# Low parts of one weight tile in eight by an accumulating DMA in a transformer block kernel

## The chip, the cores and the metric

The kernel runs on one core of one Trainium2 chip. The metric is the device time of one execution in microseconds. Two runs of the kernel before took 1663.89 and 1665.68 us, a median of 1664.79 us. The engines are named as in the profile: PE is TensorE (PEld its weight loads), DVE is VectorE, ACT is ScalarE, POOL is GpSimd, SP is SyncE, which here issues loads and stores. A name with a q behind it (SPq, ACTq) is the engine's own instruction queue.

## The reference, cut to what matters

One decoder layer for 256 tokens of width 2048, all in float32. Every large step is a product of the activations with a weight matrix; the parts between them are small.

```
h = rmsnorm(x, ln_mix)                               # x: 256 x 2048
z = h @ w_in                                         # 2048 x 14336: u,v | q,k,v | gates
y_a = spatial_gating_mixer(u, v) @ w_proj_a          # 2048 x 2048
y_b = moba_mixer(q, k, v, rel_bias) @ w_proj_b       # 2048 x 2048
x = x + (sigmoid(g_a) * y_a + sigmoid(g_b) * y_b) @ w_out
h = rmsnorm(x, ln_mlp)
x = x + square(relu(h @ w_up)) @ w_down              # 2048 x 8192, 8192 x 2048
out = rmsnorm(x, ln_final)
```

## The kernel before

All weights together are cut into 288 tiles of 512 rows by 512 columns (1 MB in float32, held as 128 partitions by 2048 elements). Four tiles one below the other make a chunk, which is one product over 2048 rows; there are 72 chunks. Their order is fixed by the list `chunks`: three products (k, q, v) for each of four groups of heads, then the gate of the attention branch (gb), its projection (pb), the spatial branch's v (gv) and u, its projection (pa) and gate (ga), the output projection (wo), and four times four chunks of the MLP's first matrix (up) and four of its second (dn). Tiles are counted through from 0 to 287; tile j belongs to chunk j // 4.

Each float32 weight w is used as two parts of a shorter type (float32r), w = hi + lo, and the activations likewise. A product then takes three matmuls in place of one: hi weights with hi activations, lo weights with hi activations, hi weights with lo activations. In `rows` (L141 to L143), where the activations are the stationary operand, the three follow each other for each block of 128 rows, so that the second matmul of a tile already reads lo. In `cols` (L158), where the weights are stationary, four matmuls with hi and hi, four with hi and the low activations, and then four with lo follow each other for each block of 128 rows, so the first eight matmuls of a tile read hi alone.

`WeightStream` brings the tiles. `load` (L56) issues a DMA from SP into a tile `wraw`, of which there are four buffers. `split` makes hi by a copy with rounding on ACT (L72) and lo by a subtraction on DVE (L73); there are three buffers of `whi` and three of `wlo`. So the split of tile j waits until PE is done with tile j - 3, and the load of tile j + 4 waits until the split of tile j has read `wraw`. The last tile alone puts its parts into separate tiles named `spare`. `get`, called ahead of each tile's matmuls, issues loads up to five tiles ahead and splits up to two tiles ahead. The small work between the products (attention heads, norms, gates) is issued in stages, one or two per weight tile, by `tick`. A scheduler of the language sets the final order of each engine's instructions and the semaphores between engines; each engine then runs its own list in order.

Of the kernel before, what the change touches and what calls it, by code (L numbers as in the profile page):

```python
# [12 lines left out]
F32 = mybir.dt.float32  # L13
F32R = mybir.dt.float32r
AF = mybir.ActivationFunctionType
ALU = mybir.AluOpType
AX = mybir.AxisListType

P = 128
D = 2048  # L20
T = 256
NT = T // P
KT = D // P
# [5 lines left out]
EPS = 1e-6  # L29
NEG = -1e30  # L30
SCALE = P ** -0.5
CH = 512
KG = 4
RV = 384


class WeightStream:
    """Weights in tiles of KG*128 rows by CH columns, laid out as in_tiles() does, each split exactly into two float32r parts:
    w = hi + lo. Loads and splits are issued ahead of the products that use them."""

    def __init__(self, nc, pool, chunks, ahead=2, loads_ahead=5):
        self.nc, self.pool = nc, pool
# [17 lines left out]
    def split(self, pieces=None, between=None):  # L60
        j = self.n_split
        t = self.raw.pop(j)
        if j == len(self.tiles) - 1 and self.spare:
            hi, lo = self.spare
        else:
            hi = self.pool.tile([P, KG, CH], F32R, tag="whi", name=f"whi{j}", bufs=3)
            lo = self.pool.tile([P, KG, CH], F32R, tag="wlo", name=f"wlo{j}", bufs=3)
        for a, b in pieces or (((0, 2), (2, 4)) if j < 6 else ((0, KG),)):
            if between:
                between(a, b)  # L70
            s = slice(a, b)
            self.nc.scalar.activation(hi[:, s], t[:, s], AF.Copy)  # L72
            self.nc.vector.tensor_tensor(lo[:, s], t[:, s], hi[:, s].bitcast(F32), ALU.subtract)  # L73
        self.parts[j] = (hi, lo)
        self.n_split += 1

# [11 lines left out]
def block_kernel(ctx, tc, x, x_t, ln_mix, w_in, v_gain, w_sp, b_sp, w_pa, w_pb, w_out, rel_bias,  # L88
# [23 lines left out]
        chunks += [(w_up, 0, b * D + c * CH) for c in range(4)]  # L112
        chunks += [(w_down, b * D, c * CH) for c in range(4)]

# [1 line left out]
    tasks = deque()  # L116

    def tick(limit=2):
# [10 lines left out]
    stream = WeightStream(nc, wpool, chunks)  # L129

    def rows(acts, name):
        """[tokens, CH] = acts.T @ W over 2048 rows, both token tiles."""
        ps = psum.tile([P, NT, CH], F32, tag="mm", name=name, bufs=2)
        for i in range(KT // KG):
            hi, lo = stream.get()
            for kk in range(KG):
                k = i * KG + kk
                ah, al = acts(k)
                for t in range(NT):
                    s = slice(t * P, (t + 1) * P)  # L140
                    nc.tensor.matmul(ps[:, t], ah[:, s], hi[:, kk], start=k == 0, stop=False)  # L141
                    nc.tensor.matmul(ps[:, t], ah[:, s], lo[:, kk], start=False, stop=False)  # L142
                    nc.tensor.matmul(ps[:, t], al[:, s], hi[:, kk], start=False, stop=k == KT - 1)  # L143
            if i < KT // KG - 1:
                tick()
        return ps

    def cols(acts, name):
        """[CH as 4 x 128, tokens] = W.T @ acts over 2048 rows."""
        ps = psum.tile([P, CH // P, T], F32, tag="mm", name=name, bufs=2)  # L150
        for i in range(KT // KG):
            hi, lo = stream.get()
            for kk in range(KG):
                k = i * KG + kk
                ah, al = acts(k)
                for j, (w, a) in enumerate(((hi, ah), (hi, al), (lo, ah))):
                    for n in range(CH // P):
                        nc.tensor.matmul(ps[:, n], w[:, kk, n * P : (n + 1) * P], a,  # L158
                                         start=k == 0 and j == 0 and n % 2 == 0,
                                         stop=k == KT - 1 and j == 2, skip_group_check=True)  # L160
            if i < KT // KG - 1:
                tick()
        return ps

# [1 line left out]
    ident = const.tile([P, P], F32, name="ident")  # L166
    make_identity(nc, ident)
    ones = const.tile([P, P], F32, name="ones")
# [17 lines left out]
    first = [((0, 1), (1, 2), (2, 3), (3, 4))] * 2 + [((0, 2), (2, 4))] * 2  # L186
# [4 lines left out]
    hh = hold.tile([P, KT, T], F32R, tag="h", name="hh", bufs=2)  # L191
# [10 lines left out]
        split_x(k)  # L202

    def rsqrt(dst, s, n, scale=1.0):
        """dst = (scale * s + EPS) ** -0.5, the table's root refined by a Newton step."""
        v = const.tile([P, n], F32, tag="rs_v", name="rs_v", bufs=2)
        y = const.tile([P, n], F32, tag="rs_y", name="rs_y", bufs=2)
        q = const.tile([P, n], F32, tag="rs_q", name="rs_q", bufs=2)
        nc.vector.tensor_scalar(v, s, scale, EPS, op0=ALU.mult, op1=ALU.add)
        nc.scalar.activation(y, v, AF.Sqrt)  # L210
        nc.vector.reciprocal(y, y)
        nc.vector.tensor_mul(q, y, y)
        nc.vector.tensor_mul(q, q, v)
        nc.vector.tensor_scalar(q, q, -0.5, 1.5, op0=ALU.mult, op1=ALU.add)
        nc.vector.tensor_mul(dst, y, q)

    def row_of(r, name):
        """r [token, 2] on every partition as a row [*, 256]."""
        ps = psum.tile([P, T], F32, tag="tp", name=name + "p", bufs=2)
        for t in range(NT):  # L220
            dg = const.tile([P, P], F32, tag="diag", name="dg", bufs=2)
            nc.vector.tensor_scalar(dg, ident, r[:, t : t + 1], None, op0=ALU.mult)
            nc.tensor.matmul(ps[:, t * P : (t + 1) * P], ones, dg, start=True, stop=True)
        rb = const.tile([P, T], F32, tag="rb", name=name, bufs=2)
        nc.vector.tensor_copy(rb, ps)
        return rb
# [22 lines left out]
    tasks.append(first_norm())  # L249

    def split_t(dst_h, dst_l, k0, src):
        """Two transposed blocks [128, 2, 256] in PSUM -> hi and lo parts of k0, k0 + 1."""
        nc.scalar.activation(dst_h[:, k0 : k0 + 2], src, AF.Copy)
        nc.vector.tensor_tensor(dst_l[:, k0 : k0 + 2], src, dst_h[:, k0 : k0 + 2].bitcast(F32),
                                ALU.subtract)

    def transpose_pair(src, k, name):
        """Blocks k, k + 1 (of 128 columns) of src [tokens, ...] -> PSUM [128, 2, 256]."""
        tp = psum.tile([P, 2, T], F32, tag="tp", name=name, bufs=2)
        for a in range(2):  # L260
            for t in range(NT):
                nc.tensor.transpose(tp[:, a, t * P : (t + 1) * P],
                                    src[:, t, (k + a) * P : (k + a + 1) * P], ident)
        return tp

# [1 line left out]
    bh = bl = None  # L267
    with tc.tile_pool(name="attn", bufs=1) as at:
        rv = at.tile([HEADS, RV], F32, tag="pt", name="rv", bufs=2)
# [53 lines left out]
            nc.scalar.activation(bh[:, h], pv, AF.Copy)  # L323
            nc.vector.tensor_tensor(bl[:, h], pv, bh[:, h].bitcast(F32), ALU.subtract)

        hacts = lambda k: (hh[:, k], hl[:, k])  # noqa: E731

        def scale_cols(ps, name):
            dst = at.tile([P, 4, T], F32, tag=name[:2], name=name, bufs=2)
# [23 lines left out]
                tasks.append(head(c, j, qt, kt, vt, bt))  # L353
            tick()

# [1 line left out]
        m = hold.tile([P, NT, D], F32, tag="m", name="m", bufs=1)  # L357
        for c in range(4):
            ps = rows(hacts, f"gb{c}")
# [4 lines left out]
        drain()  # L364

    with tc.tile_pool(name="gmlp", bufs=1) as gp:
# [1 line left out]
        for c in range(4):  # L368
            ps = rows(lambda k: (bh[:, k], bl[:, k]), f"pb{c}")
            for t in range(NT):  # L370
                s = m[:, t, c * CH : (c + 1) * CH]
                nc.vector.tensor_tensor(s, s, ps[:, t], ALU.mult)

# [1 line left out]
        gain = gp.tile([P, GROUPS], F32, name="gain")  # L375
        nc.sync.dma_start(gain, v_gain)
        gv = gp.tile([P, NT, D], F32, tag="gv", name="gv", bufs=1)
# [62 lines left out]
            for t in range(NT):  # L440
                nc.scalar.activation(pa[:, t, c * CH : (c + 1) * CH], ps[:, t], AF.Copy)

# [1 line left out]
        mh = ab.tile([P, KT, T], F32R, tag="ab", name="mh", bufs=2)  # L444
        ml = ab.tile([P, KT, T], F32R, tag="ab", name="ml", bufs=2)

# [13 lines left out]
                nc.vector.tensor_tensor(m[:, t, s], m[:, t, s], g[:, t], ALU.add)  # L460
            tasks.append(merged(c))

# [1 line left out]
    lnp = const.tile([P, KT], F32, name="lnp")  # L464
    nc.sync.dma_start(lnp, ln_mlp)
    x1 = hold.tile([P, NT, D], F32, tag="m", name="x1", bufs=1)
# [7 lines left out]
    r2 = const.tile([P, NT], F32, name="r2")  # L474

    def add_rows(ps, t, s, sums=None):
        """x1 += ps in columns s of token tile t; sums gets the sum of the squares."""
        xs = x1[:, t, s]
        nc.vector.tensor_tensor(xs, xs, ps, ALU.add)
        if sums is not None:  # L480
            jk = const.tile([P, CH], F32, tag="junk", name="jk", bufs=2)
            nc.scalar.activation(jk[:, : s.stop - s.start], xs, AF.Square, accum_out=sums)
# [24 lines left out]

    ab_open.close()

# [1 line left out]
    mlp = ctx.enter_context(tc.tile_pool(name="mlp", bufs=1))  # L511
    lnf = mlp.tile([P, D], F32, name="lnf")
    nc.sync.dma_start(lnf, bass.AP(tensor=ln_final.tensor, offset=ln_final.offset,
# [1 line left out]
    for b in range(DFF // D):  # L515
        hid = []
        for c in range(4):
# [10 lines left out]
                nc.scalar.activation(q, v, AF.Square)  # L528
                nc.vector.tensor_tensor(tl[:, s], q, th[:, s].bitcast(F32), ALU.subtract)
            hid.append((th, tl))  # L530
        acts = lambda k: (hid[k // 4][0][:, k % 4], hid[k // 4][1][:, k % 4])  # noqa: E731
        last = b == DFF // D - 1
        for c in range(3 if last else 4):
            ps = rows(acts, f"dn{b}_{c}")
# [5 lines left out]
                else:  # L540
                    add_rows(ps[:, t], t, s)

# [1 line left out]
    spare = [hold.tile([P, KG, CH], F32R, tag="h", name=f"spare{i}", bufs=2) for i in range(2)]  # L544
    stream.spare = tuple(spare)
    out_v = out.rearrange("(t p) d -> t p d", p=P)
# [42 lines left out]


def in_tiles(w):
    """[rows, cols] as [row tile, column tile, 128, KG, CH]: each weight tile in one piece."""
    r, c = w.shape
    return np.asarray(w).reshape(r // (KG * P), KG, P, c // CH, CH).transpose(0, 3, 2, 1, 4)


def _onehot():
    """Which bucket a distance of 255 - m falls in, for m < 256; the rest is masked."""
    n = np.arange(256)
    half = BUCKETS // 2  # L600
    large = half + (np.log(np.maximum(n, 1).astype(np.float32) / np.float32(half))
# [45 lines left out]
```

## Time and profile before

| what | value |
|---|---|
| runs before, median of 2 | 1664.79 us (1663.89 to 1665.68) |
| span of the profiled execution | 1662.5 us |
| PE busy | 1651.6 us, 99% |
| DVE busy | 850.9 us, 51% |
| ACT busy | 688.8 us, 41% |
| POOL busy | 4.3 us |
| read from HBM | 311.50 MB, 190 GB/s over the span |
| hardware DMA queue (SP) | 53.9% of 16 engines' time |
| queue of DMAs issued by POOL | 32 packets, 0.01 MB |

The span runs from the first to the last instruction of one execution that the hardware profiler took, 2.3 us less than the median of the runs. Busy time of an engine says how long its instructions ran, not whether anybody waited for them; the waits and the timeline say that. A load's time to landing is counted from its issue to the moment its semaphore says that the data is there. The share of the DMA engines is a mean over the whole span.

### The profile page before, as it was taken

The page shows a single profiled execution, that of the slowest core. Times are in us where ns is not written, and L with a number is a line of the kernel's source. Part 1 is how long each engine was busy: PE and PEld are TensorE (multiplying, and loading weights), DVE is VectorE, ACT ScalarE, POOL GpSimd, SP SyncE. Part 2 cuts the span into 40 slices and gives each one's busy share as a digit, 9 for nine tenths or more (in the row PEclk, how much of TensorE's full clock was granted, in tenths as well). Part 3 has the DMA queues.
Part 4 walks back from the last instruction along what each step waited for, and adds up shares of the span by engine and source line. Part 5 has one row for each costly group of instructions (what it writes and reads, how often), then busy time and mean ns, then how long its engine had stood idle before and what let it go on. Part 6 is the DMA issues. An engine that isn't in the chain of part 4 may idle for free.

```text
span 1662.5 us, 22670 instructions
## 1 busy us (share of the span) xinstructions
PE 1651.6 (99%) x9988; PEld 1483.7 (89%) x9988; DVE 850.9 (51%) x726; ACT 688.8 (41%) x614; POOL 4.3 (0%) x11
## 2 busy tenths in 40 slices
PE   9999999999999999999999999999999999999997
PEld 9899999888888899888888999889988998899986
DVE  7545544544445555544555555444545455445554
ACT  7444343443334443434444444334443443334432
POOL 0000000000000000000000000000000000000000
PEclk9999999999999999999999999999999999999999
DMA  9855444465555554555465554555555555555551
GB/s 317 254 193 187 165 178 170 159 223 185 200 192 189 192 199 169 184 191 202 178 234 189 210 178 178 202 189 191 178 186 194 190 190 178 201 181 186 190 183 74
DMA packets 51762, 317.16 MB, mean 191 GB/s; under 512 B 5664, under 2 KB 10832, under 8 KB 14928
## 3 DMA queue, kind: packets, MB, share of 16 engines
q1 hardware_dynamic: 51632, 315.71, 53.9%
q8 instruction: 78, 1.28, 0.3%
q14 instruction: 20, 0.16, 0.0%
q0 software_dynamic: 32, 0.01, 0.0%
HBM read 311.50 MB, written 4.19 MB: 190 GB/s over the span
## 4 chain that ended last, share of the span: by engine, by line
PE 99%; DMA 0%; DVE 0%; ACT 0%; issue 0%; DVEq 0%; POOL 0%; POOLq 0%; ACTq 0%
PE up L158 22%; PE dn L142 7%; PE dn L143 7%; PE dn L141 7%; PE kt L158 6%; PE qt L158 6%; PE u L158 6%; PE v L142 2%; PE wo L143 2%; PE ga L143 2%; PE gb L141 2%; PE wo L141 2%; PE ga L141 2%; PE wo L142 2%; PE pa L141 2%; PE v L141 2%
## 5 line engine op out<-in xcount | busy, mean ns | idle before, releaser
L73 DVE TENSOR_TENSOR wlo<-wraw,whi 128x2048 fp32r<-128x2048 f32 (+2 forms) x297 | 658.9, 2219 | 644.8 <-ACT whi L72 644.8
L72 ACT ACTIVATE whi<-wraw 128x2048 fp32r<-128x2048 f32 (+2 forms) x297 | 551.5, 1858 | 832.6 <-PE up L158 188.9
L141 PE MATMUL dn<-whi,hh 128*128 128x512 f32 x480 | 186.8, 389 | 0.0
L142 PE MATMUL dn<-wlo,hh 128*128 128x512 f32 x480 | 186.8, 389 | 0.0
L143 PE MATMUL dn<-whi,hl 128*128 128x512 f32 x480 | 186.7, 389 | 0.0
L158 PE MATMUL up<-h2h,whi 128*128 128x256 f32 x1024 | 164.7, 283 | 0.0
L158 PE MATMUL up<-h2l,whi 128*128 128x256 f32 x1024 | 164.6, 283 | 0.0
L158 PE MATMUL up<-h2h,wlo 128*128 128x256 f32 x1024 | 164.6, 283 | 0.0
L158 PEld LDWEIGHTS up<-h2h,whi 128*128 128x128 f32 x1024 | 141.5, 192 | 0.3
L158 PEld LDWEIGHTS up<-h2h,wlo 128*128 128x128 f32 x1024 | 141.3, 192 | 0.0
L158 PEld LDWEIGHTS up<-h2l,whi 128*128 128x128 f32 x1024 | 141.3, 192 | 0.0
L143 PEld LDWEIGHTS dn<-whi,hl 128*128 128x128 f32 x480 | 90.1, 188 | 18.7
L141 PEld LDWEIGHTS dn<-whi,hh 128*128 128x128 f32 x480 | 90.1, 188 | 18.6
L142 PEld LDWEIGHTS dn<-wlo,hh 128*128 128x128 f32 x480 | 90.1, 188 | 18.6
L141 PE MATMUL gb<-whi,hh 128*128 128x512 f32 x128 | 50.6, 395 | 0.0
L141 PE MATMUL wo<-whi,mh 128*128 128x512 f32 x128 | 50.6, 395 | 0.0
L141 PE MATMUL ga<-whi,hh 128*128 128x512 f32 x128 | 50.4, 394 | 0.0
L141 PE MATMUL v<-whi,hh 128*128 128x512 f32 x128 | 50.0, 391 | 0.0
L141 PE MATMUL pa<-whi,ah 128*128 128x512 f32 x128 | 50.0, 391 | 0.0
L143 PE MATMUL wo<-whi,ml 128*128 128x512 f32 x128 | 50.0, 390 | 0.0
L142 PE MATMUL v<-wlo,hh 128*128 128x512 f32 x128 | 50.0, 390 | 0.0
L143 PE MATMUL ga<-whi,hl 128*128 128x512 f32 x128 | 49.9, 390 | 0.0
(180 smaller groups left out, 2394.8 us busy)
## 6 DMA issues: line engine op xcount, KB each, us to landing
wraw<-in_w_in SPq DMA_DIRECT2D x108, 1024.0 KB, 4.8
wraw<-in_w_up SPq DMA_DIRECT2D x64, 1024.0 KB, 4.8
wraw<-in_w_down SPq DMA_DIRECT2D x64, 1024.0 KB, 4.8
wraw<-in_w_pb SPq DMA_DIRECT2D x16, 1024.0 KB, 4.8
wraw<-in_w_pa SPq DMA_DIRECT2D x16, 1024.0 KB, 4.8
wraw<-in_w_out SPq DMA_DIRECT2D x16, 1024.0 KB, 4.8
wraw<-in_w_in SPq DMA_DIRECT2D x8, 256.0 KB, 4.7
wraw<-in_w_in SPq DMA_DIRECT2D x4, 512.0 KB, 7.5
```

The source lines that it names most:

```text
L72: self.nc.scalar.activation(hi[:, s], t[:, s], AF.Copy)
L73: self.nc.vector.tensor_tensor(lo[:, s], t[:, s], hi[:, s].bitcast(F32), ALU.subtract)
L141: nc.tensor.matmul(ps[:, t], ah[:, s], hi[:, kk], start=k == 0, stop=False)
L142: nc.tensor.matmul(ps[:, t], ah[:, s], lo[:, kk], start=False, stop=False)
L143: nc.tensor.matmul(ps[:, t], al[:, s], hi[:, kk], start=False, stop=k == KT - 1)
L158: nc.tensor.matmul(ps[:, n], w[:, kk, n * P : (n + 1) * P], a, start=k == 0 and j == 0 and n % 2 == 0, stop=k == KT - 1 and j == 2, skip_g ...
```

## The change

For every tile j with j % 8 == 7 the low part is made in another way: ACT writes the negative of the high part into `wlo` (a second copy with rounding, with scale -1), and a DMA issued by POOL reads the same 1 MB of weights from HBM a second time and adds it to what is in `wlo`. For the other tiles nothing changes. The docstrings and comments that the changed file leaves out, and the five lines that it adds, move line numbers behind the edit up by five: the subtraction on DVE is L78 there, the matmuls of `rows` L146 to L148, those of `cols` L163.

```diff
             s = slice(a, b)
             self.nc.scalar.activation(hi[:, s], t[:, s], AF.Copy)
-            self.nc.vector.tensor_tensor(lo[:, s], t[:, s], hi[:, s].bitcast(F32), ALU.subtract)
+            if j % 8 == 7:
+                self.nc.scalar.activation(lo[:, s], t[:, s], AF.Copy, scale=-1.0)
+                w, r0, c0 = self.tiles[j]
+                self.nc.gpsimd.dma_start(lo[:, s], w[r0 // (KG * P), c0 // CH][:, s], accum_op=ALU.add)
+            else:
+                self.nc.vector.tensor_tensor(lo[:, s], t[:, s], hi[:, s].bitcast(F32), ALU.subtract)
         self.parts[j] = (hi, lo)
```

There are 36 such tiles, each the last of its chunk: 14 in chunks that `cols` computes, 22 in chunks that `rows` computes, the last tile of the program (287) among these.

On ACT, around the split of tile 199 (a tile of `cols`, in the second chunk of the MLP's second group; the number behind whi, wlo and wraw is that of the tile), the list before reads:

```order
L527 ACTIVATE hh1_0_8727<-v_8735 128x512
L528 ACTIVATE q_8736<-v_8735 128x512
L72 ACTIVATE whi199_8798<-wraw199_8619 128x2048
L72 ACTIVATE whi200_8852<-wraw200_8673 128x2048
L72 ACTIVATE whi201_8906<-wraw201_8742 128x2048
```

And with the change:

```order
L532 ACTIVATE hh1_0_8751<-v_8759 128x512
L533 ACTIVATE q_8760<-v_8759 128x512
L72 ACTIVATE whi199_8822<-wraw199_8643 128x2048
L74 ACTIVATE wlo199_8823<-wraw199_8643 128x2048
L72 ACTIVATE whi200_8877<-wraw200_8697 128x2048
L72 ACTIVATE whi201_8931<-wraw201_8766 128x2048
```

The negative copy stands behind the high part of the same tile and ahead of the next tile's.

On ACT, around the split of tile 215 (a tile of `rows`, in the second chunk of the second product of the same group), the list before reads:

```order
L72 ACTIVATE whi213_9527<-wraw213_9435 128x2048
L72 ACTIVATE whi214_9560<-wraw214_9465 128x2048
L72 ACTIVATE whi215_9590<-wraw215_9495 128x2048
L72 ACTIVATE whi216_9620<-wraw216_9525 128x2048
L72 ACTIVATE whi217_9650<-wraw217_9558 128x2048
```

And with the change:

```order
L72 ACTIVATE whi213_9553<-wraw213_9461 128x2048
L72 ACTIVATE whi214_9586<-wraw214_9491 128x2048
L74 ACTIVATE wlo215_9617<-wraw215_9521 128x2048
L72 ACTIVATE whi215_9616<-wraw215_9521 128x2048
L72 ACTIVATE whi216_9647<-wraw216_9551 128x2048
L72 ACTIVATE whi217_9677<-wraw217_9584 128x2048
```

Here the negative copy stands ahead of the high part of its own tile.

On POOL, whose list before holds no DMA but the load of one small vector, the same part of the program now reads (wlo is written, the weights of w_up and w_down are read):

```order
L76 DMA wlo191_8444<-in_w_down 128x2048
L76 DMA wlo199_8823<-in_w_up 128x2048
L76 DMA wlo207_9286<-in_w_up 128x2048
L76 DMA wlo215_9617<-in_w_down 128x2048
L76 DMA wlo223_9864<-in_w_down 128x2048
```

PE's and SP's lists keep their order; the 36 subtractions are gone from DVE's list.

## Rows read from the trace of the kernel before

**Rows 1.** The page's part 1, busy time, share and instructions of each engine.

```profile
span 1662.5 us, 22670 instructions
PE 1651.6 (99%) x9988; PEld 1483.7 (89%) x9988; DVE 850.9 (51%) x726; ACT 688.8 (41%) x614; POOL 4.3 (0%) x11
```

**Rows 2.** The waits of PE, all of them: total us, times, longest.

```profile
PE wps L175 <- DVE ssq L472: 1.1, 1, 1.1
PE kt L158 <- ACT whi L72: 1.0, 1, 1.0
```

**Rows 3.** Waits of all engines, three rows of DVE, ACT and SP.

```profile
DVE wlo L73 <- ACT whi L72: 644.8, 271, 8.8
...
ACT whi L72 <- PE up L158: 188.9, 52, 3.8
...
SPq L56 <- DVE wlo L73: 1341.5, 261, 8.6
```

**Rows 4.** Timeline around tile 199 (cols): start, duration, engine, line.

```profile
1143.76 1.92 ACT L72 ACTIVATE whi<-wraw 128x2048 fp32r<-128x2048 f32 x1 [1.81 <-issue]
1149.52 1.92 ACT L72 ACTIVATE whi<-wraw 128x2048 fp32r<-128x2048 f32 x1 [3.84 <-PE up L158]
...
1145.71 2.29 DVE L73 TENSOR_TENSOR wlo<-wraw,whi 128x2048 fp32r<-128x2048 f32 x1 [2.31 <-ACT whi L72]
...
1155.51 0.64 PE L158 MATMUL up<-h2h,whi 128*128 128x256 f32 x4
...
1156.47 0.64 PE L158 MATMUL up<-h2h,wlo 128*128 128x256 f32 x4
```

**Rows 5.** Timeline around tile 215 (rows): ACT, DVE, SP and PE.

```profile
1234.78 1.92 ACT L72 ACTIVATE whi<-wraw 128x2048 fp32r<-128x2048 f32 x1 [3.52 <-PE dn L143]
...
1236.72 2.29 DVE L73 TENSOR_TENSOR wlo<-wraw,whi 128x2048 fp32r<-128x2048 f32 x1 [3.15 <-ACT whi L72]
...
1239.04 5.77 SPq L56 DMA_DIRECT2D wraw<-in_w_down  x2
...
1245.46 0.39 PE L141 MATMUL dn<-whi,hh 128*128 128x512 f32 x1
1245.68 0.39 PE L142 MATMUL dn<-wlo,hh 128*128 128x512 f32 x1
```

**Rows 6.** The DMA view of 1234 to 1246 us, rates in 40 slices of 0.3 us.

```profile
GB/s 0 109 109 410 218 437 410 437 410 410 246 218 82 0 0 0 0 0 0 0 164 218 218 300 382 437 437 437 437 410 55 27 0 0 0 0 0 0 382 27
```

**Rows 7.** The page's parts 3 and 6: DMA queues; issues, KB each, us to landing.

```profile
q1 hardware_dynamic: 51632, 315.71, 53.9%
...
wraw<-in_w_up SPq DMA_DIRECT2D x64, 1024.0 KB, 4.8
...
rv_d<-rv SPq DMA_DIRECT2D x1, 2048.0 KB, 25.5
...
lnm<-in_ln_mix POOLq DMA_DIRECT2D x1, 8.0 KB, 3.5
```

**Rows 8.** Timeline of the first microseconds, POOL's one DMA.

```profile
1.32 0.67 POOL L179 DMA_DIRECT2D lnm<-in_ln_mix  x1 [0.32 <-issue]
```

**Rows 9.** Timeline around the split of tile 7, ACT and SP.

```profile
34.59 0.69 SPq L285 DMA_DIRECT2D rv_d<-rv  x1
...
36.43 1.92 ACT L72 ACTIVATE whi<-wraw 128x2048 fp32r<-128x2048 f32 x1 [1.94 <-PE qt L158]
```

**Rows 10.** Stretches: length, busy us (instructions) of five engines, clock, DMA share, GB/s.

```profile
41.50:83.00 41.50, 41.50 (x257) 37.27 (x256) 21.19 (x26) 17.60 (x18) 0.00 (x0) 1.00 0.88 255
...
1654.00:1656.00 2.00, 0.00 (x0) 0.00 (x0) 1.03 (x6) 0.71 (x3) 0.00 (x0) 1.00 0.00 0
1656.00:1658.00 2.00, 0.00 (x0) 0.00 (x0) 1.86 (x7) 0.72 (x1) 0.00 (x0) 0.59 0.00 0
1658.00:1660.00 2.00, 0.00 (x0) 0.00 (x0) 0.02 (x1) 0.00 (x0) 0.00 (x0) 0.50 0.98 358
```

## The prediction

> **What bounds the kernel now.** I read the busy times first, then PE's waits, then the waits of the engines that feed PE, then the timeline of two tiles that the change touches, and last the DMA views. PE is busy for 1651.6 of 1662.5 us [rows 1]. Its waits sum to 2.1 us [rows 2]. So the kernel is bound by PE's matmuls from end to end, and nothing on ACT, DVE or the DMA engines holds PE up. Those engines wait on PE instead: ACT stands idle up to 3.8 us for the release of a weight buffer, and DVE 644.8 us in total for ACT [rows 3]. The timeline shows how early the parts of a tile are ready. Tile 215's parts are begun at 1234.78, when PE is done with tile 212, and its first matmul starts at 1245.46 [rows 5]. DVE ends lo at 1236.72 + 2.29 = 1239.01. PE reads lo first at 1245.68, so 6.7 us lie between. For tile 199 lo ends at 1145.71 + 2.29 = 1148.00 and is read first at 1156.47 [rows 4], 8.5 us later. A gain for PE is not to be had here: all that PE doesn't fill is 10.9 us, 0.7%. The question is whether the new way of making lo fits into the time that a tile has.
>
> **What the change removes.** 36 subtractions of 2.29 us [rows 4, 5], 82 us of DVE's busy time. DVE already idles; worth 0 to PE. SP's load into a freed `wraw` buffer is released by DVE's subtraction now (261 waits, [rows 3]) and by ACT's second copy after, at about the same moment, since 1.92 us take the place of 2.29 us: nothing.
>
> **What it adds on ACT.** 36 copies of 1.92 us, if a copy with a scale costs as the one without (the same operation and shape, [rows 4, 5]): 69 us, 688.8 becomes about 758 us. Behind the extra copy stands the next tile's high part. At tile 199 the two copies end at 1143.76 + 2 x 1.92 = 1147.6, and the next copy starts at 1149.52 [rows 4], so the idle time hides it. At tile 215 the negative copy goes first and hi comes 1.92 us later, at about 1238.6, still 6.8 us ahead of 1245.46 [rows 5]. If that cover were gone, 36 x 1.92 = 69 us would be the most it could cost. I take 0.
>
> **What it adds on POOL and the DMA engines.** This is the term that decides. The DMA may be issued only when ACT has written the negative copy, and PE waits for its landing before the first matmul with lo; PE's list is in order, so everything behind waits too. The window for it:
> - In `cols` (tile 199) the negative copy comes second and ends at 1147.6. The first matmul with lo is at 1156.47: 8.9 us.
> - In `rows` (tile 215) the negative copy comes first and ends at about 1236.5 (0.2 us before hi did, since the last matmul with lo of tile 212 is the last but one). The first matmul with lo is at 1245.68: 9.2 us.
>
> How long does such a DMA take? No row of before shows one, so I build it from the nearest. POOL's issue of its one DMA took 0.67 us [rows 8]. The load of tile 219 is issued at 1239.04 [rows 5]; its bytes move in 12 slices of 0.3 us, from 1240.0 to 1243.6, at up to 437 GB/s [rows 6]. So some 1.0 us pass ahead of the first byte, 3.6 us move 1 MB, and with 4.8 us to landing [rows 7] 0.2 us are left behind the last. At the top rate 1 MB takes 1.05 / 0.437 = 2.4 us. An adding DMA has to read the weights and also read what stands in lo, and write the sum.
> - Lower end: it costs as a load from SP, with POOL's issue, 0.7 + 4.8 = 5.5 us. It lands 3.4 us early; cost 0. Less than 0 is excluded, as PE has nothing to gain.
> - Two passes of 1 MB through the DMA engines: 0.7 + 1.0 + 3.6 + 2.4 + 0.2 = 7.9 us alone. But the freed `wraw` buffer starts a load of another 1 MB within 2 us on either side of it, and the engines are then shared: up to 2.4 us more, 10.3 us.
> - Three passes, if the write counts too or the add slows the stream by as much: 12.7 us.
> - Upper end: the slowest large DMA of the trace, `rv_d`, needs 25.5 us for 2 MB [rows 7].
>
> I take the mean of the two middle values, 11.5 us, because they are built from the load of the same shape, the nearest row, while `rv_d` moves another pattern. That is 2.6 us too late in `cols` and 2.3 us in `rows`. The delay isn't made up later, as PE has no slack, and it isn't carried into the next tile, whose parts are ready. The last tile (287) has its own buffers and no load beside it; I count it at nothing. So 14 x 2.6 + 21 x 2.3 = 84.7 us.
>
> One tile stands apart. Tile 7 is split at 36.43 while `rv_d`, issued at 34.59 [rows 9], runs for 25.5 us, and the DMA engines are 88% busy until 83 us [rows 10]. Its DMA may come later by anything from 0 to 16 us (25.5 less its window); I add 5 us. Later loads have time: the load of tile 219 lands at 1243.8, and its split follows four tiles of 5.44 us behind 1234.78, at 1256.5. The 36 DMAs add 36 x 2 x 2.98 = 215 us of all 16 engines' time (0.539 x 1662.5 us for 301 pieces of 1 MB is 2.98 us each, [rows 7]), so their share goes from 53.9% to about 67%, which loads can bear.
>
> Sum: 1662.5 + 84.7 + 5 = 1752 us of span, and with the 2.3 us that the median lies above the span, **1754 us**.
>
> A rule on the sharing. In the trace 1 MB moves at up to 437 GB/s while one load is under way [rows 6], but no row shows two large DMAs of two queues beside each other. The Trainium skill ("DMA: Bandwidth & Descriptors", section "Issuing engines are not separate DMA queues") says that DMAs from sync and gpsimd end up on the same 16 engines and interleave, whoever issued them. By that rule the load takes its 2.4 us from the adding DMA; if the queues had engines of their own, two passes would take 7.9 us and nothing would be lost. I keep the sharing, and the runs of before can't show it.
>
> **The rivals.**
> - *It lands in time (no change).* The add rides along with the load and costs no pass of its own, or the load beside it takes less than I count. Up to 10.0 us of duration the loss stays under 0.95 us a tile, 35 x 0.95 = 33 us, 2% of the time and about what a measurement of this kernel can tell from no change. For it: the lower end lies here, so do two passes without the load beside them (7.9 us), and two passes with it miss it by 0.3 us. Against: the load beside it is there at each of the 36 tiles. Time: 1665 us if the DMA lands inside its window. The Trainium skill ("DMA: Bandwidth & Descriptors", section "Anatomy of one DMA — SWDGE (gpsimd) path") gives for a DMA from gpsimd about 2.0 us and bytes / 436e3, an estimate of 4.4 us for 1 MB and 6.8 us if 2 MB count; by that rule this rival holds. No run here shows it, and it is for plain moves.
> - *It lands far too late.* The adding DMA runs at the pace of `rv_d`, 25.5 us for 1 MB read and 1 MB read and written. Then PE waits 16.6 us at 14 tiles and 16.3 us at 21, 575 us, 2240 us. It decides from 13.7 us of duration on (4.6 us a tile, 1830 us). Such waits may also lower PE's clock: after PE's last matmul the granted clock is 1.00 for about 2 us, then 0.59 and 0.50 of 2.4 GHz, the level of 1.2 GHz [rows 10]. What a product costs at that level no row shows; I leave it to the range. For this rival: nothing in the trace shows the adding part. Against: the load of the same shape moves in 3.6 us.
> - *DVE's relief counts (faster).* Only if PE's 2.1 us of waits hid more; the whole idle time of PE gives 1652 us, inside 2%.
>
> **How the numbers follow.** In time or nearly (up to 10.0 us): 0.32. The forecast (10.0 to 13.7 us, 1698 to 1830 us): 0.40. Far too late: 0.27, spread over 1830 to 2240 us. Faster by over 2%: 0.01. That gives faster 0.01, same 0.32, slower 0.67. The range goes from 1660 us (the first case with a little noise) to 1960 us, which is a duration of 17.4 us, 8.3 us late at 35 tiles, and leaves out about half of the last rival. The forecast's own range is 1698 to 1830 us.
>
> **What would show it.** Right: PE's waits list its matmuls with lo waiting for the DMA into `wlo`, some 35 times, 2 to 3 us each, 85 us in all; 36 issues from POOL of 1024 KB with 10 to 13 us to landing; ACT at about 758 and DVE at about 769 us busy; the DMA share near 67% (of the old span); granted clock still 1.00. Wrong: no such waits, with a landing under 9 us (then the add is free); or landings over 14 us and a lower clock behind each wait (then the adding rate is the cause, not the sharing); or ACT's high parts late, which would put the loss on the extra copy.

## The result, and the profile after

The changed kernel takes 1721.06 us (median of two runs, 1720.02 and 1722.10) against 1664.79 us before: a ratio of 1.0337, with a 95% interval from 1.0318 to 1.0357. It is slower, by 56 us. The forecast was 1754 us, in a range from 1660 to 1960.

The page of the changed kernel, parts 1 and 3, busy time of the engines and DMA queues (packets, MB, share of 16 engines):

```profile
span 1718.3 us, 22753 instructions
...
PE 1667.2 (97%) x9988; PEld 1490.4 (87%) x9988; DVE 769.7 (45%) x690; ACT 753.4 (44%) x650; POOL 37.1 (2%) x47
...
q1 hardware_dynamic: 51632, 315.71, 51.8%
q0 software_dynamic: 5216, 37.76, 11.4%
```

Against [rows 1] DVE is 81 us less busy and ACT 65 us more, close to the forecast (82 and 69). The queue of POOL's DMAs now carries the 37.8 MB that are read twice. PE's busy time has grown by 15.6 us for the same 9988 matmuls; the clock, below, has a part in that. The rest of the 55.8 us of span is in PE's waits, of which the longest are (total us, times, longest; in the changed file L163 and L147 are the matmuls of `cols` and those of `rows` with lo):

```profile
PE up L163 <- DMA wlo<-in_w_up: 17.7, 8, 2.4
PE qt L163 <- DMA wlo<-in_w_in: 15.9, 2, 13.9
PE gv L147 <- DMA wlo<-in_w_in: 2.2, 2, 1.9
PE gb L147 <- DMA wlo<-in_w_in: 2.0, 2, 1.6
...
PE dn L147 <- DMA wlo<-in_w_down: 0.7, 3, 0.3
```

Where [rows 2] had two waits of 1 us, PE now waits for the adding DMA 40.0 us in all (the five rows above and four more groups of 0.2 to 0.6 us). These 40.0 us and the 15.6 us of longer busy time make up 55.6 of the 55.8 us. Three things can be read from the rows. The eight changed tiles of up wait 2.2 us each. One tile of qt waits 13.9 us; it is tile 7. The tiles of dn hardly wait at all in this list.

The DMA view of the changed kernel says why (issues, KB each, median us to landing):

```profile
wlo<-in_w_in POOLq DMA_DIRECT2D x14, 1024.0 KB, 10.7
wlo<-in_w_up POOLq DMA_DIRECT2D x8, 1024.0 KB, 11.1
wlo<-in_w_down POOLq DMA_DIRECT2D x7, 1024.0 KB, 9.2
...
spare<-in_w_down POOLq DMA_DIRECT2D x1, 1024.0 KB, 7.9
```

The same DMA lands after 11.1 us in products with stationary weights (`cols`: up), after 9.2 us in those with stationary activations (`rows`: dn), and after 7.9 us at the last tile, beside which nothing is loaded any more. The timeline of a tile of up and of a tile of dn, those of [rows 4] and [rows 5] (ACT, SP, POOL, PE):

```profile
1183.30 1.90 ACT L74 ACTIVATE wlo<-wraw 128x2048 fp32r<-128x2048 f32 x1
...
1185.22 0.33 SPq L56 DMA_DIRECT2D wraw<-in_w_up  x1
...
1185.49 0.87 POOL L76 DMA_DIRECT2D wlo<-in_w_up  x1 [46.20 <-ACT wlo L74]
...
1193.71 0.64 PE L163 MATMUL up<-h2l,whi 128*128 128x256 f32 x4
...
1196.28 0.74 PE L163 MATMUL up<-h2h,wlo 128*128 128x256 f32 x4 [1.93 <-DMA wlo<-in_w_up]
...
1277.01 1.92 ACT L74 ACTIVATE wlo<-wraw 128x2048 fp32r<-128x2048 f32 x1 [3.29 <-PE dn L147]
...
1279.21 0.86 POOL L76 DMA_DIRECT2D wlo<-in_w_down  x1 [44.60 <-ACT wlo L74]
...
1280.75 0.33 SPq L56 DMA_DIRECT2D wraw<-in_w_down  x1
...
1288.42 0.50 PE L147 MATMUL dn<-wlo,hh 128*128 128x512 f32 x1
```

At the tile of up the negative copy is the last to read `wraw`, so its end at 1185.2 releases two DMAs at once: the load into the freed buffer goes out at 1185.22, ahead of the adding DMA at 1185.49. The adding DMA lands 10.7 us later, and PE starts with lo at 1196.28, 1.93 us late. At the tile of dn the adding DMA goes out at 1279.21 and the load only at 1280.75, after the second copy. It lands after 9.2 us, some 0.3 us after PE wants it. The load that goes out first, at up, is hardly delayed: it takes 5.4 us to landing, 4.8 in the kernel before [rows 7]. The one that goes out second, at dn, takes 8.9 us.

Tile 7 stands apart again. The DMA view of 40 to 41 us, in which its adding DMA is issued:

```profile
DMA packets 95, 0.10 MB, mean 97 GB/s; under 512 B 0, under 2 KB 95, under 8 KB 95
...
wraw<-in_w_in SPq DMA_DIRECT2D x1, 1024.0 KB, 30.1
wlo<-in_w_in POOLq DMA_DIRECT2D x1, 1024.0 KB, 23.2
```

All packets of this microsecond are small ones of the store `rv_d`, issued at 34.3 us. The adding DMA lands after 23.2 us, the load of tile 10, issued at 36.2 us, after 30.1.

The third cost is the clock. Stretches of the changed kernel (length, busy us of PE, PEld, DVE, ACT, POOL with counts, granted clock, DMA share, GB/s), at tile 7 and at the first changed tile of up:

```profile
50.00:52.00 2.00, 0.00 (x0) 0.00 (x0) 1.74 (x1) 0.23 (x1) 0.00 (x0) 1.00 0.85 96
52.00:54.00 2.00, 0.00 (x0) 0.00 (x0) 0.55 (x1) 0.00 (x0) 0.00 (x0) 0.62 0.84 97
...
66.00:68.00 2.00, 2.00 (x11) 2.00 (x11) 0.00 (x0) 0.00 (x0) 0.00 (x0) 0.50 1.00 422
68.00:70.00 2.00, 2.00 (x13) 2.00 (x12) 0.00 (x0) 0.00 (x0) 0.00 (x0) 0.61 0.99 392
70.00:72.00 2.00, 2.00 (x15) 1.86 (x14) 0.69 (x2) 1.12 (x1) 0.00 (x0) 1.00 1.10 409
...
1006.00:1008.00 2.00, 0.00 (x0) 0.00 (x0) 1.49 (x1) 0.48 (x1) 0.00 (x0) 1.00 0.95 315
1008.00:1010.00 2.00, 1.61 (x7) 1.61 (x8) 0.80 (x1) 0.00 (x0) 0.00 (x0) 0.56 0.85 307
1010.00:1012.00 2.00, 2.00 (x13) 2.00 (x12) 0.00 (x0) 0.00 (x0) 0.00 (x0) 0.59 0.74 295
1012.00:1014.00 2.00, 2.00 (x19) 2.00 (x19) 0.00 (x0) 0.00 (x0) 0.00 (x0) 1.00 0.53 217
```

After PE has stood still the granted clock is 0.50, the level of 1.2 GHz, also for the first matmuls that follow: 11 matmuls in 2 us where 19 are counted at the full clock. At tile 7 that lasts until about 69.5 us. Behind a wait of only 2.4 us in up it comes too, at three of the eight tiles; behind waits of 1.9 to 2.36 us at the other five it doesn't.

When the starts of the same matmuls in the two traces are subtracted, the 55.7 us split so: 16.7 at tile 7, 24.1 at the eight tiles of up (4.1 each at the three with the lower clock, 2.2 to 2.6 at the others), 2.2 at the other tile of qt, 4.2 at one tile each of gb and gv, and 8.5 scattered over the rest, mostly 0.3 to 0.7 us a tile; the tiles of dn lose 0.35 to 0.56 us each, and those of ga and wo nothing. At the tile of gb the loads of `ws` and `bs` go out beside the DMA as well; why the one of gv lands late, after 10.9 us, isn't known.

### The profile page after: what moved, and what is told of

Read it like the earlier page. It is cut to its first block, busy times and chain, and to the rows that moved or that the text cites. A ratio compares the mean times of both kernels' runs of the same rounds, so it can differ in the third digit from the quotient of the medians.

```text
span 1718.3 us, 22753 instructions
## 1 busy us (share of the span) xinstructions
PE 1667.2 (97%) x9988; PEld 1490.4 (87%) x9988; DVE 769.7 (45%) x690; ACT 753.4 (44%) x650; POOL 37.1 (2%) x47
## 3 DMA queue, kind: packets, MB, share of 16 engines
q0 software_dynamic: 5216, 37.76, 11.4%
## 5 line engine op out<-in xcount | busy, mean ns | idle before, releaser
L78 DVE TENSOR_TENSOR wlo<-wraw,whi 128x2048 fp32r<-128x2048 f32 (+2 forms) x262 | 578.9, 2210 | 701.5 <-ACT whi L72 701.5
L147 PE MATMUL dn<-wlo,hh 128*128 128x512 f32 x480 | 187.6, 391 | 1.0 <-DMA wlo<-in_w_down 0.7
L146 PE MATMUL dn<-whi,hh 128*128 128x512 f32 x480 | 186.8, 389 | 0.0
L148 PE MATMUL dn<-whi,hl 128*128 128x512 f32 x480 | 186.8, 389 | 0.0
L163 PE MATMUL up<-h2h,wlo 128*128 128x256 f32 x1024 | 167.0, 286 | 17.7 <-DMA wlo<-in_w_up 17.7
L163 PE MATMUL up<-h2l,whi 128*128 128x256 f32 x1024 | 166.4, 285 | 0.0
L163 PE MATMUL up<-h2h,whi 128*128 128x256 f32 x1024 | 166.1, 285 | 0.0
L163 PEld LDWEIGHTS up<-h2h,wlo 128*128 128x128 f32 x1024 | 142.9, 194 | 19.3 <-DMA wlo<-in_w_up 19.3
L163 PEld LDWEIGHTS up<-h2l,whi 128*128 128x128 f32 x1024 | 143.1, 194 | 0.0
L163 PEld LDWEIGHTS up<-h2h,whi 128*128 128x128 f32 x1024 | 142.8, 194 | 0.3
L147 PEld LDWEIGHTS dn<-wlo,hh 128*128 128x128 f32 x480 | 90.1, 188 | 22.3 <-DMA wlo<-in_w_down 4.0
L146 PEld LDWEIGHTS dn<-whi,hh 128*128 128x128 f32 x480 | 90.1, 188 | 18.7
L148 PEld LDWEIGHTS dn<-whi,hl 128*128 128x128 f32 x480 | 90.1, 188 | 18.5
L74 ACT ACTIVATE wlo<-wraw 128x2048 fp32r<-128x2048 f32 x35 | 66.8, 1910 | 57.5 <-PE dn L147 21.8
L163 PE MATMUL qt<-hh,wlo 128*128 128x256 f32 x256 | 42.6, 290 | 15.9 <-DMA wlo<-in_w_in 15.9
L147 PE MATMUL gv<-wlo,hh 128*128 128x512 f32 x128 | 50.0, 391 | 2.2 <-DMA wlo<-in_w_in 2.2
L147 PE MATMUL gb<-wlo,hh 128*128 128x512 f32 x128 | 50.0, 391 | 2.0 <-DMA wlo<-in_w_in 2.0
L146 PE MATMUL gb<-whi,hh 128*128 128x512 f32 x128 | 50.6, 396 | 0.0
L163 PEld LDWEIGHTS qt<-hh,wlo 128*128 128x128 f32 x256 | 36.5, 198 | 16.3 <-DMA wlo<-in_w_in 16.3
L146 PE MATMUL wo<-whi,mh 128*128 128x512 f32 x128 | 50.6, 395 | 0.0
L147 PE MATMUL pb<-wlo,bh 128*128 128x512 f32 x128 | 50.0, 391 | 0.4 <-DMA wlo<-in_w_pb 0.4
## 6 DMA issues: line engine op xcount, KB each, us to landing
wlo<-in_w_in POOLq DMA_DIRECT2D x14, 1024.0 KB, 10.7
wlo<-in_w_up POOLq DMA_DIRECT2D x8, 1024.0 KB, 11.1
```

Source lines behind the costliest of these rows:

```text
L74: self.nc.scalar.activation(lo[:, s], t[:, s], AF.Copy, scale=-1.0)
```

## The experiments

Theory A: the loss is nothing but late landings of the adding DMA, which shares the DMA engines with whatever is loaded beside it. At `cols` tiles the order of the two copies makes that worst, at tile 7 the long store `rv_d`. Rival B: the DMA is slow beside products with stationary weights as such. Rival C: the copies and the added traffic cost something by themselves.

**The copy alone, without the DMA.**

```diff
-                self.nc.gpsimd.dma_start(lo[:, s], w[r0 // (KG * P), c0 // CH][:, s], accum_op=ALU.add)
+                self.nc.vector.tensor_tensor(lo[:, s], t[:, s], lo[:, s].bitcast(F32), ALU.add)
```

> ScalarE writes the negative high part into lo as in the change, and VectorE adds the weights to it from the buffer, with no DMA: the term of the extra copy alone. Theory A: 0, 1665 us within 2 us. Rival C: several us more than 1665, up to 69 us if nothing hid the copies.

Measured: 1664.62 us, a ratio of 0.9999 (0.9990 to 1.0008). The page and the line group of the copies:

```profile
PE 1651.4 (99%) x9988; PEld 1483.9 (89%) x9988; DVE 851.9 (51%) x726; ACT 753.5 (45%) x650; POOL 3.9 (0%) x11
...
L74 ACT ACTIVATE wlo<-wraw 128x2048 fp32r<-128x2048 f32 x35 | 66.8, 1910 | 57.6 <-PE dn L146 21.8 <-PE v L146 7.6 <-PE pb L146 6.6
```

ACT does the whole extra work, 66.8 us at 1.91 us a copy, and PE's busy time is that of [rows 1]. The copies cost nothing, as forecast.

**The negative copy first, everywhere.** A one-column copy from lo into hi keeps the scheduler from placing hi ahead of it.

```diff
+                self.nc.scalar.activation(lo[:, s], t[:, s], AF.Copy, scale=-1.0)
+                self.nc.scalar.activation(hi[:, 0, :1], lo[:, 0, :1], AF.Copy)
+                self.nc.gpsimd.dma_start(lo[:, s], w[r0 // (KG * P), c0 // CH][:, s], accum_op=ALU.add)
+                self.nc.scalar.activation(hi[:, s], t[:, s], AF.Copy)
```

> The negative copy is forced ahead of the high part at all 36 tiles, as it already stands in products with stationary activations (a one-column copy from lo into hi orders the two). Theory A (the DMA is late in products with stationary weights because it is issued 1.9 us later there and together with the load into the same freed buffer): the landings of these 14 tiles fall from about 11 to about 9.3 us, the waits of up (17.7 us) and of the second qt (2.0 us) go, and with them the clock drops behind three of them; tile 7's wait stays. 1721 - 24 (up) - 2 (qt) = about 1695 us. Rival B (the DMA itself is slower beside matmuls with stationary weights, whatever is loaded): landings stay at 11 us, the window grows by some 1.5 us, the waits shrink from 2.2 to about 0.7 us: about 1706 us.

Measured: 1699.44 us, 1.0214 (1.0189 to 1.0240). Its DMA view and the head of PE's waits:

```profile
wlo<-in_w_up POOLq DMA_DIRECT2D x8, 1024.0 KB, 9.2
wlo<-in_w_down POOLq DMA_DIRECT2D x7, 1024.0 KB, 9.1
```

```profile
PE qt L165 <- DMA wlo<-in_w_in: 13.1, 1, 13.1
PE gb L149 <- DMA wlo<-in_w_in: 3.4, 2, 3.2
PE dn L149 <- DMA wlo<-in_w_down: 2.4, 7, 0.4
```

The landings of up fall from 11.1 to 9.2 us, those of dn, and the waits of up are gone from the list. Theory A holds against rival B, under which 11 us should have stayed. The total is 4 us above the expectation: one tile of gb now costs 6.3 us (in the change 2.0), with a stretch of lower clock behind its 3.2 us wait.

**Tile 7 left to VectorE.**

```diff
-            if j % 8 == 7:
+            if j % 8 == 7 and j > 7:
```

> Tile 7 is split on VectorE as before, the other 35 tiles as in the change. Theory A: the 13.9 us wait of qt and the half clock behind it go, 16.7 us in all: about 1704 us. Rival (the delay of tile 7 is only moved to the next tile of the crowded first 83 us): little changes, 1715 to 1721 us.

Measured: 1702.19 us, 1.0232 (1.0215 to 1.0249), 18.9 us less than the change. The delay isn't moved to a neighbour: the next changed tile, 15, loses nothing against the kernel before.

**Both edits.**

> Both edits. Theory A: only the scattered 0.3 to 2 us at tiles of the other products remain, some 12 us: about 1678 us. Rival B with tile 7 gone: about 1689 us. Rival C (a general cost of the extra copies and of 38 MB more on the DMA engines, spread over the run): 1690 us or more, with no waits of PE for the DMA that explain it.

Measured: 1682.25 us, 1.0107 (1.0092 to 1.0122). The matmul starts show 5.1 us at a tile of gb and 4.0 at one of gv, both with a lower clock behind the wait, 0.3 to 0.9 us at most other tiles in `rows`, and nothing at those in `cols`. The profiled execution is the slowest of the four, 1686.13 us. The median is 4 us above theory A's number, 7 below rival B's and 8 below rival C's; and PE's list has 11.4 us of waits for the DMA, where C had none.

**The load beside it sent behind it.** The loads into the freed buffer go through POOL's queue, after the adding DMA.

```diff
-            self.nc.sync.dma_start(t[:, a:b], src[:, a:b])
+            (self.nc.gpsimd if j % 8 == 3 and j > 8 else self.nc.sync).dma_start(t[:, a:b], src[:, a:b])
```

> The change with the loads of the tiles j % 8 == 3 (those that go into the buffer that the split of a changed tile frees) issued from GpSimd, behind the adding DMA on the same queue, in place of SyncE. Theory A (the load beside it takes its time): the landings at products with stationary weights fall from 11 to about 8.5 us, the waits of up nearly go. Rival B (they are slow beside such products whatever is loaded): they stay at 11 us. Tile 7's wait stays in both.

Measured: 1683.23 us (one run). The DMA view:

```profile
wlo<-in_w_in POOLq DMA_DIRECT2D x14, 1024.0 KB, 8.0
...
wraw<-in_w_up POOLq DMA_DIRECT2D x8, 1024.0 KB, 9.6
wlo<-in_w_up POOLq DMA_DIRECT2D x8, 1024.0 KB, 8.0
...
wlo<-in_w_down POOLq DMA_DIRECT2D x7, 1024.0 KB, 8.0
```

Without the load the DMA lands after 8.0 us in both kinds of product, as at the last tile of the change (7.9). So the difference between 8.0 and 9.2 or 11.1 us is the load beside it. That load now takes 9.6 us to landing at up, in place of the 5.4 above, and nobody waits for it. PE's only long wait left is tile 7's, 14.5 us.

**The same, with tile 7 left to VectorE.**

> The loads of tiles j % 8 == 3 behind the adding DMA on GpSimd's queue, and tile 7 split on VectorE: the other 35 adding DMAs in the windows of the change. Theory A: nothing but about 2 us at two crowded tiles (gb, gv) is left, 1667 us. Rival C (a cost of the copies and of the added DMA traffic by itself): 1675 us or more.

Measured: 1667.58 us, 1.0013 (1.0003 to 1.0022). 35 of the 36 adding DMAs still run in the windows of the change, and 2.0 us are left against the kernel before beside it (1665.61 us). The copies and 35 of the 36 MB of added traffic are all there, so rival C falls.

**The DMA without the add.**

```diff
-                self.nc.gpsimd.dma_start(lo[:, s], w[r0 // (KG * P), c0 // CH][:, s], accum_op=ALU.add)
+                self.nc.gpsimd.dma_start(lo[:, s], w[r0 // (KG * P), c0 // CH][:, s])
```

> The change with the DMA only writing the weights into lo, without adding: the low part of these tiles is then the whole weight. Two passes (reading the old content costs one more pass of 2.4 us): landings fall by about 2.4 us, to 6.8 us (rows) and 8.6 us (cols), the waits of up go. Three passes: they fall by about 4.8 us. If the add rides along for nothing: they stay at 9.2 and 11 us.

Measured: 1676.26 us (one run). The DMA view:

```profile
q0 software_dynamic: 5216, 37.76, 6.1%
...
wlo<-in_w_up POOLq DMA_DIRECT2D x8, 1024.0 KB, 7.0
wlo<-in_w_down POOLq DMA_DIRECT2D x7, 1024.0 KB, 5.1
...
spare<-in_w_down POOLq DMA_DIRECT2D x1, 1024.0 KB, 5.1
```

Alone the add costs 7.9 - 5.1 = 2.8 us, a little over one pass of 2.4 us; three passes would have cost 4.8 us alone. Beside a load it costs 4.1 us in both kinds (11.1 - 7.0 and 9.2 - 5.1), which by the numbers expected lies nearer to three passes. The time that the packets of POOL's queue took speaks for two: 11.4% of 1718.3 us in the change and 6.1% of 1674.6 us here, 196 and 102 us for the same 5216 packets, a factor of 1.9. So the add is about one more pass; that this pass is the reading of the old content is argued and not shown. What remains of the time, 11.5 us, is again tile 7: even the plain DMA lands 10.5 us late there.

**The MLP only, and the MLP with an own buffer for these lo tiles.** In both only the tiles from 160 on are changed, and the hidden layer's low part has five buffers in place of six. The second issues the same copies and DMAs two tiles earlier; of its edit the part that does this:

```diff
+            if j % 8 == 7 and j >= 160:
+                lo = self.own.tile([P, KG, CH], F32R, tag="wlo8", name=f"wlo{j}", bufs=1)
+            else:
+                lo = self.pool.tile([P, KG, CH], F32R, tag="wlo", name=f"wlo{j}", bufs=3)
```

> The DMA makes the low part only in the MLP (16 tiles, j >= 160), in the buffers of the change; one buffer fewer for the hidden layer's low part, which nothing waits for. Control for the next run. Theory A: the waits of the MLP's tiles as in the change, 24 us in up and some 4 us in dn: about 1693 us.

> As the run before, but these 16 tiles put lo into a buffer of their own, so the negative copy and its DMA are issued about two tiles (11 us) earlier. The same copies, bytes and DMAs. Theory A (only the window is too short): no wait is left, 1665 us within 3 us. Rival C (copies, DMA traffic or slower loads cost by themselves): as far above 1665 us as they cost, up to the 1693 us of the run before.

Measured: 1691.36 us, 1.0157 (1.0140 to 1.0174), without the own buffer, and 1665.26 us, 1.0003 (0.9993 to 1.0012), with it. PE's waits in the second, all of them:

```profile
PE kt L166 <- ACT whi L75: 1.4, 1, 1.4
PE wps L183 <- DVE ssq L480: 1.1, 1, 1.1
```

The DMAs still take 10.1 us (up) and 8.8 us (dn) to land in this run, but the window is longer than that. The same bytes and copies then cost nothing. It doesn't beat the kernel before either, since PE had nothing to gain.

The first of the two runs also shows that the length of a wait alone does not decide on the clock. It fell at four of the eight tiles of up: behind waits of 2.4 us at two, and behind 1.9 us at two others, while it stayed at 1.00 behind 2.4 us at three and 1.95 us at one. A wait of 1.93 us that ends at 1538.03:

```profile
1536.00:1538.00 2.00, 0.10 (x1) 0.00 (x0) 1.35 (x1) 0.61 (x1) 0.00 (x0) 1.00 0.93 311
1538.00:1540.00 2.00, 1.97 (x9) 1.98 (x10) 0.94 (x1) 0.00 (x0) 0.00 (x0) 0.52 0.92 320
```

**The store `rv_d` moved, earlier and later.**

```diff
-            for _ in range(4):
+            for _ in range(1):
```

> The change with the 2 MB store of the bias rows (rv_d, 25 to 29 us of small packets) issued three stages earlier, ahead of tile 7's load, so that most of it is over when tile 7's DMA starts at about 40 us. Theory A (tile 7 waits 13.9 us because its DMA shares the engines with this store): its landing falls from 23.2 to about 12 to 16 us and its wait to 3 to 7 us; in all some 10 us less than the change. Rival (the crowd of loads at the start does it): landing stays above 20 us.

Measured: 1727.95 us (one run), a miss. The scheduler moved the store only 5 us, to 29.5 us, but ahead of the loads of tiles 7 and 8. These came late themselves, and PE waited 10.5 us for tile 7's high part and 8.2 us for its DMA (landing 14.5 us). The stretches around it show the store at work:

```profile
30.00:35.00 5.00, 5.00 (x44) 5.00 (x44) 5.00 (x7) 3.77 (x4) 0.00 (x0) 1.00 0.72 77
35.00:40.00 5.00, 5.00 (x44) 5.00 (x43) 3.05 (x8) 0.00 (x0) 0.00 (x0) 1.00 0.83 95
40.00:45.00 5.00, 5.00 (x44) 5.00 (x44) 1.71 (x3) 0.00 (x0) 0.00 (x0) 1.00 0.84 95
...
55.00:60.00 5.00, 0.29 (x1) 0.29 (x2) 0.00 (x0) 2.25 (x2) 0.00 (x0) 0.50 1.01 424
```

For some 20 of the 24.5 us that the store takes, all DMAs together move 77 to 95 GB/s; behind it 424. The loads and the DMA that are issued beside it come late.

```diff
-            for _ in range(4):
+            for _ in range(7):
```

> The change with the store of the bias rows issued behind the load of tile 12, after tile 7's DMA has started, in place of ahead of the load of tile 10; nothing else moves. Theory A (this store starves the other transfers for its 25 us): tile 7's DMA lands in 9 to 12 us in place of 23.2, its wait falls from 13.9 to under 3 us, and the run is some 12 to 16 us shorter than the change (1721), unless loads behind the store now come late and PE waits there in its place. Rival (the loads of the start delay tile 7): its landing stays above 20 us.

Measured: 1712.91 us (one run), 8 us less than the change and short of the 12 to 16 expected. The DMA view of 42 to 43 us has tile 7's DMA:

```profile
wlo<-in_w_in POOLq DMA_DIRECT2D x1, 1024.0 KB, 11.4
```

It lands after 11.4 us instead of 23.2, and the wait falls to 2.2 us. So the store is the cause of most of tile 7's wait. Some of the gain is given back at tile 15, where PE now waits 5.5 us. The DMA lands there after 11.5 us, as in the change (11.1); but PE wants lo 6.4 us after the negative copy's end and not 11.5 us. ACT comes to that copy later in the order of PE's work than it did; whether the late bias rows do that was not tried.

## Why the prediction was right or wrong

**Right: the bound and the place.** PE is the bound, and the loss is PE waiting with its first matmul with lo for the DMA. The copies (0, measured 0) and VectorE's relief (0; DVE is 81 us less busy and nobody gains) came as written.

**Right: the windows of the two tiles read, and the DMA alone.** 8.9 and 9.2 us were read as the windows; from the copy's end at 1185.2 to where lo would have been read, at 1193.71 + 0.48 = 1194.2, are 9.0 us. Two passes alone were put at 7.9 us; the last tile measures 7.9 and the run with the load behind 8.0. That this fits to a tenth is luck: its part without the add was put at 5.5 us and measures 5.1, and the second pass was put at 2.4 us and measures 2.8.

**Mis-sized: the duration beside a load.** The step that failed is "I take the mean of the two middle values, 11.5 us", for both kinds of tile. The add is about two passes (2.8 us over the plain DMA), so the value for two, 10.3 us, was the one to start from, and the load beside it isn't a fixed 2.4 us: it costs 1.2 us in `rows`, where it starts 1.5 us behind the DMA, and 3.1 us in `cols`, where it goes out first. The forecast had seen that the negative copy comes second in `cols`, that ACT's second copy frees `wraw`, and that the load starts within 2 us on either side. It did not go on to ask which of the two DMAs goes out first, and gave both kinds of tile the same 11.5 us. Landings count from POOL's issue, 0.3 us after the copy's end from which the windows count. So 11.1 us against a window of 9.0 is 2.4 us too late (2.2 us on average at up), and 9.2 against 9.2 is 0.3 us. The 21 tiles of `rows`, put at 48 us, cost 11.5 us in all, 4.2 of them at the two odd tiles of gb and gv.

**Mis-sized: one window for all tiles of a kind.** The 13 tiles of `cols` without tile 7, put at 34 us, cost 28 us, and only those of up and qt in full. Those of u and kt land after 10.5 to 11.4 us and hardly wait (0.6 us for one of u). The trace shows why: between the copy's end and the first matmul with lo PE also works through 16 small matmuls of the attention (`pv`, `sc`) at kt and 8 of the gating (`sv`) at u, so the window is 11.5 and 10.8 us there. At three of the four tiles of ga and wo, which lose nothing, it is 10.2 us for the same reason.

**Too small: tile 7 and the clock.** Tile 7 was given 2.6 us and 5 more, of a range from 0 to 16; it cost 16.7. The mechanism named, the store beside it, is the one that the late store shows. The trace of the kernel before already had its size. In its DMA view of 36.4 to 36.6 us a load of 1 MB, issued 1.9 us behind the store, takes 26.1 us and not the 4.8 of [rows 7]:

```profile
wraw<-in_w_in SPq DMA_DIRECT2D x1, 1024.0 KB, 26.1
```

The granted clock was forecast to stay at 1.00. In the change it fell after waits of 2.4 us. Three tiles of up lose 1.7 us beyond their wait by it, where the others lose 0.25 us, and tile 7 loses 2.7 us (seven groups of about 0.85 us in place of 0.48). These errors work against the ones above, so that 1754 and 1721 us lie nearer to each other than the parts of the sum do; that is luck.

**The rivals.** *In time* was nearly true of most tiles in `rows`, and with a longer window it was true of all 16 of the MLP. *Far too late* was true of one tile only by its landing (23.2 us), and by another mechanism than the rival's: the adding DMA has no slow pace of its own, it ran beside `rv_d`. As for the rule of the Trainium skill on sharing ("DMA: Bandwidth & Descriptors", section "Issuing engines are not separate DMA queues"), the runs agree: with the load out of the way, 8.0 us in place of 9.2 and 11.1. Its fit for a DMA from gpsimd (section "Anatomy of one DMA — SWDGE (gpsimd) path") gave estimates of 4.4 and 6.8 us; measured from POOL's issue to landing, with no load beside, are 5.1 us plain and 7.9 us with the add. The measurement decides.

## What to carry to other kernels

Work that is taken from an idle engine gains nothing when another engine is the bound, and its replacement is judged by its latency against the time between the release of the buffer and the first use, not by its busy time. A DMA that adds cost about a second pass here (7.9 us in place of 5.1), and when the instruction that releases it also frees a load buffer, it shares the engines with that load: let the adding DMA go first, or give it a buffer that is free earlier. Look for long transfers in small packets, such as the 2 MB store here (under 2 KB each), since a load issued beside it landed after 26 to 30 us here, in place of 4.8.

## What the runs showed of the hardware

The granted clock fell to 0.50 behind PE waits as short as 1.9 us (two tiles of up in the run with the MLP only), and stayed at 1.00 behind others of 2.4 us of the same kind in the same run. One store of 2 MB took 24.5 to 31 us in these runs; for 15 to 20 us of it all DMAs together moved about 77 to 102 GB/s, at a DMA share of 0.72 to 0.88. The same 1 MB adding DMA landed in anything from 7.9 to 23.2 us in the change, by what ran beside it. When an adding DMA and a load went out within 2 us of each other, the one that went second was delayed more: with the load first, at the tile of up, the load took 5.4 us and the adding DMA 10.7; with the adding DMA first, at the tile of dn, it took 9.2 us and the load 8.9. By themselves they take 4.8 and 8.0 us.
